# Attention in another order with the output projection and the layer norms between its halves, and feed-forward tiles at other addresses

## The chip, the cores and the metric

One core of one Trainium2 chip runs the whole program. TensorE (PE) multiplies, VectorE (DVE), ScalarE (ACT) and GpSimd (POOL) do the rest, SyncE (SP) issues the DMAs. A kernel's time is device microseconds of one execution; the profile comes from one execution with its own time. Operands of matmuls stand in SBUF, where each of 128 partitions has its own bytes; "an address" below is a byte offset in every partition. Results go to PSUM.

## The reference

One layer of a decoder trunk: 2048 tokens, width 1024. An input projection feeds four causal mixers of 256 columns each (RWKV-7, dilated attention, Mamba-2 SSD, HGRN2). Their joined output goes through an output projection and a layer norm, then through a feed-forward part of 4096 columns and a second layer norm:

```python
  proj = x @ W_in[l]
  y    = concat(rwkv7, dilated_attn, ssd, hgrn2) @ W_out[l]
  x    = LayerNorm(alpha * x + y)
  x    = LayerNorm(alpha * x + relu(x @ W_up)^2 @ W_down)
```

The attention has 4 heads of 64 and three branches, with window 128, 512 and 2048 and dilation 1, 4 and 16. Each branch takes every d-th token as a row of its own, cuts it into blocks of 128, and a block attends to itself and to the block before it, with a bias that falls linearly with distance. The branches are merged by their softmax sums:

```python
    s = einsum(qb, kb) * (Dh ** -0.5) + bias
    m = max(s); p = exp(s - m); l = sum(p)
    o = einsum(p, vb) / l
```

## The kernel before

**Arithmetic.** Every large product is taken in three: an operand is split into a high and a low part (tiles ending in `h` and `l`, from `split`, `split_to` or `tsplit`), and high x high, high x low and low x high are summed in PSUM. A matmul of this kind has 512 moving columns and takes its 128x128 stationary operand in a load of its own (PEld).

**Order.** The program is written in one order and a scheduler, when the program is built, sets from it the order of each engine's instructions; the chip then works each engine's list off in turn, waiting on semaphores. Tiles come from pools; a tile with `bufs=n` has n places and waits for the reader of the one n tiles back. Six PSUM banks (`bank` in the profile) are given out by name with `slot`, two more are the pool `pd` (tile `mm`).

**Stages.** First the input projection and the mixers RWKV, HGRN and SSD run, to about 1265 us; the change leaves them. Then:

- *Attention* (`attn_units`, `attn_unit`): 48 units, one for each branch, remainder and block of 128 queries. A unit has two halves (`par`, two heads each). A half multiplies queries and keys (4 heads' worth in two calls, `kT`, `qT`; 128 or 256 keys), adds the bias and takes the maximum on DVE (`aS`, `aml`), takes the exponential on ACT, transposes on PE, copies to `aPT` on ACT or DVE, multiplies with the values (`av`, called PV below) and copies to `ao`, which a DMA stores to `od`. The first 12 units use other PSUM banks (`"1"`) and stand in the program while the last mixer still runs.
- *First part of the output projection* (`out_part(t)`, 16 tiles of 128 tokens): loads three mixers' output `ym`, transposes it (6 transposes), splits it to `yh`, `yl`, multiplies with 6 of the 8 row tiles of the weights (36 matmuls), adds alpha times x in `zt`, and stores that to `zF`.
- *Closing part* (`out_final(t)`): loads the three branches (`mo`), merges them (`attn_merge`, on POOL and DVE with `me`, `md`, `mw`), transposes and splits to `yah`, `yal`, multiplies with the last two row tiles (12 matmuls), does the layer norm (`stat`, and on ACT a square that is only wanted for its sum, into `junk`), stores it to `x1`, transposes it (8 transposes) into `x1t` and stores that to `x1T`, from which the feed-forward part reads.
- *Feed-forward up* (`ffn_up(hf, ...)`, two halves of 1024 tokens): seven products in place of eight, after Strassen, for 16 steps `s`, with 84 matmuls each. `ffn_x(hf)` builds the seven sums of activations `X` once for each half of the tokens, from loads `xr`; `ffn_w(s)` builds the sums of weights (`wr`, `wh`, `wl`). The finished columns go to `HT`.
- *Feed-forward down* (`ffn_down`): 3072 matmuls and the second layer norm.

The body (lines 1403 to 1424 of the kernel before) puts these in the order: units 12 to 47; parts 0 to 7; then, for t from 0 to 7, final t and part 8 + t; then the feed-forward part, with finals 8 to 15 behind the steps 1 to 8 of its first half. The scheduler weaves part of this: in the trace, parts 0 to 7 stand among the halves, and so do some finals.

The tiles of the feed-forward part come from the pools `fx` (activations in the up stage, all operands in the down stage), `fr` (raw loads) and `fw` (weights in the up stage, from the other end of SBUF). In the built program the `fx` tiles start 160 bytes past a multiple of 2048, and the 512-byte slices of a weight tile that serve as stationary operands start 480 bytes past a multiple of 512.

## Time and profile before

| | |
|---|---|
| median of 3 runs | 3184.59 us (3163.18 to 3186.83) |
| profiled execution, own time | 3170.08 us |
| its span | 3168.3 us |
| mean granted TensorE clock | 0.938 |
| attention starts in earnest | 1268 us |
| first steady up matmuls | 1820 us |
| down stage | 2461.6 to 3158.4 us |

A row of the stretches below gives start and end, length, then for each engine its busy time with the number of its instructions, the granted clock of TensorE (1.00 is full speed), the share of time in which a DMA engine was busy, and GB/s. The busy time of PE counts overlapping matmuls once; the length of a single matmul in a row of the timeline is from its start to its last result, so the pace is read from the starts.

### The profile page before, as it was taken

The numbers are of one execution on the slowest core, as the hardware profiler recorded it, in microseconds if no ns is written. First come the engines' busy times: TensorE is split into PE (matmuls) and PEld (weight loads), VectorE is DVE, ScalarE is ACT, GpSimd is POOL, SyncE is SP. The second block draws the span as 40 slices with busy tenths as digits, with TensorE's granted clock in tenths as the row PEclk, the third lists the DMA queues.
The fourth block names the chain that finished last, engine by engine and source line by source line (L and its number), as shares of the span: only waits on it lengthen the run. The fifth ranks groups of instructions, "written<-read, shape, count | busy, mean of one in ns | idle before, by whom it ended". The sixth has DMA issues, their size and how long they took to land.

```text
span 3168.3 us, 44820 instructions
## 1 busy us (share of the span) xinstructions
PE 2988.8 (94%) x15908; PEld 2418.1 (76%) x15908; DVE 1803.9 (57%) x3577; ACT 1170.1 (37%) x2566; POOL 1063.2 (34%) x1115
## 2 busy tenths in 40 slices
PE   8899988989899998999998799998999999999998
PEld 6667777777677787777776588876888888888887
DVE  3457589687877855433354755565444333333348
ACT  3335334433443432433442454455445211111113
POOL 1333466365555645100123743344232111111111
PEclk9899898989999998798698899998999999999999
DMA  5343323432343344432256544433333622222213
GB/s 174 125 120 106 110 91 97 126 101 74 114 120 101 111 142 156 140 126 96 81 171 196 168 130 146 137 119 121 108 109 106 223 74 77 76 73 74 74 60 117
DMA packets 260145, 369.92 MB, mean 117 GB/s; under 512 B 27600, under 2 KB 145488, under 8 KB 259664
## 3 DMA queue, kind: packets, MB, share of 16 engines
q1 hardware_dynamic: 259920, 367.04, 36.8%
q8 instruction: 126, 2.06, 0.3%
q14 instruction: 99, 0.81, 0.1%
HBM read 256.12 MB, written 110.82 MB: 116 GB/s over the span
## 4 chain that ended last, share of the span: by engine, by line
PE 69%; DVE 14%; DMA 8%; issue 3%; POOL 3%; ACT 2%; SPq 1%; DVEq 0%; POOLq 0%; ACTq 0%
PE bank L112 52%; PE mm L112 15%; PE bank L157 2%; DMA xraw<-in_xT 2%; DVE hgQ L115 2%; DVE rzp L115 1%; DVE rZc L115 1%; DVE stg L128 1%; DVE wl L115 1%; DMA raw<-in_w_ch 1%; DVE xl L115 1%; DMA rLB<-lcd 1%; DMA od<-ao 1%; DMA hqP<-chF 1%; DVE hqP L115 1%
## 5 line engine op out<-in xcount | busy, mean ns | idle before, releaser
L112 PE MATMUL bank<-xl,xh 128*128 128x512 f32 x1024 | 398.3, 389 | 0.0
L112 PE MATMUL bank<-xh,xh 128*128 128x512 f32 x1024 | 398.3, 389 | 0.0
L112 PE MATMUL bank<-xh,xl 128*128 128x512 f32 x1024 | 398.0, 389 | 0.0
L112 PE MATMUL bank<-xh,wh 128*128 128x512 f32 x896 | 358.5, 403 | 12.7 <-ACT xh L135 7.6
L112 PE MATMUL bank<-xl,wh 128*128 128x512 f32 x896 | 359.8, 402 | 7.7 <-DVE xl L115 6.0
L112 PE MATMUL bank<-xh,wl 128*128 128x512 f32 x896 | 357.3, 399 | 0.0
L112 PE MATMUL mm<-xh,wh 128*128 128x512 f32 x672 | 284.0, 425 | 29.9 <-ACT xh L135 16.6
L112 PE MATMUL mm<-xl,wh 128*128 128x512 f32 x672 | 283.1, 421 | 6.3 <-POOL xl L115 3.8
L112 PE MATMUL mm<-xh,wl 128*128 128x512 f32 x672 | 279.7, 416 | 3.7 <-DVE wl L115 3.6
L112 PEld LDWEIGHTS bank<-xh,xl 128*128 128x128 f32 x1024 | 192.3, 188 | 39.9
L112 PEld LDWEIGHTS bank<-xl,xh 128*128 128x128 f32 x1024 | 192.3, 188 | 39.9
L112 PEld LDWEIGHTS bank<-xh,xh 128*128 128x128 f32 x1024 | 192.3, 188 | 39.8
L128 DVE SCALAR_TENSOR_TENSOR y<-y,bank 128x512 f32<-128x512 f32 x160 | 109.4, 686 | 196.1 <-PE bank L112 191.6
L112 PEld LDWEIGHTS bank<-xh,wh 128*128 128x128 f32 x896 | 170.3, 190 | 60.5 <-ACT xh L135 13.2
L112 PEld LDWEIGHTS bank<-xl,wh 128*128 128x128 f32 x896 | 170.6, 190 | 54.9 <-DVE xl L115 11.0
L135 ACT ACTIVATE wh<-raw 128x512 fp32r<-128x512 f32 (+1 forms) x220 | 136.9, 629 | 193.0 <-PE mm L112 85.6
L112 PEld LDWEIGHTS bank<-xh,wl 128*128 128x128 f32 x896 | 170.6, 190 | 40.2
L112 PEld LDWEIGHTS mm<-xh,wh 128*128 128x128 f32 x672 | 133.5, 199 | 69.3 <-ACT xh L135 21.6
L135 ACT ACTIVATE wh<-wr 128x512 fp32r<-128x512 f32 x160 | 100.7, 630 | 176.9 <-PE bank L112 163.0
L115 DVE TENSOR_TENSOR wl<-raw,wh 128x512 fp32r<-128x512 f32 (+1 forms) x146 | 116.7, 803 | 85.6 <-ACT wh L135 83.8
L112 PEld LDWEIGHTS mm<-xl,wh 128*128 128x128 f32 x672 | 134.1, 200 | 40.6 <-POOL xl L115 5.8
L112 PEld LDWEIGHTS mm<-xh,wl 128*128 128x128 f32 x672 | 134.1, 200 | 36.0 <-DVE wl L115 5.2
(403 smaller groups left out, 6552.4 us busy)
## 6 DMA issues: line engine op xcount, KB each, us to landing
raw<-in_w_ch SPq DMA_DIRECT2D x140, 256.0 KB, 3.0
wr<-in_w_up SPq DMA_DIRECT2D x128, 256.0 KB, 3.2
chF<-stg SPq DMA_DIRECT2D x68, 256.0 KB, 2.4
xraw<-in_xT SPq DMA_DIRECT2D x64, 256.0 KB, 3.7
HT<-u SPq DMA_DIRECT2D x64, 256.0 KB, 3.5
xr<-in_w_down SPq DMA_DIRECT2D x64, 256.0 KB, 2.9
xh<-HT SPq DMA_DIRECT2D x128, 128.0 KB, 2.5
xl<-HT SPq DMA_DIRECT2D x128, 128.0 KB, 2.6
```

The source lines that it names most:

```text
L112: self.nc.tensor.matmul(out, lhsT, rhs, start=start, stop=stop)
L115: (self.nc.gpsimd if eng == "g" else self.nc.vector).tensor_tensor(out, a, b, op=op)
L128: self.nc.vector.scalar_tensor_tensor(out, a, s, b, op0=op0, op1=op1, **kw)
L135: self.nc.scalar.activation(out, in_, AF.Copy)
L157: self.nc.tensor.transpose(out, in_, self.ident[:n, :n])
```

## The change

**Order of the units.** `attn_units` sorts them: the 16 units of dilation 16 first (each of one block; the first 12 units of all have `"1"`, as before), then dilation 1 and 4 by turns, by the stretch of 512 tokens in which they lie. So four tiles of 128 tokens have all three branches as soon as their stretch is through. The bias table `abias` gets two buffers, `aS` two in place of three.

**Weaving.** `attn_unit`, `out_mm`, `out_part` and `out_final` become generators: the first stops after each half, at its last PV matmul, a part stops 7 times, a final once. The new function `weave(units, fills)` walks through the halves and between them lets so many steps of the fills run that both end together; each step is tied behind the PV matmul of the half before (`issue_after`), so that the scheduler puts it no earlier. Four weaves: units 12 to 23 with parts 0 to 6; 24 to 31 with parts 7 to 10 and finals 0 to 3; 32 to 39 with parts 11 to 15 and finals 4 to 7; 40 to 47 with finals 8 to 11, with `ffn_x(0)` written ahead of these. Finals 12 to 15 stand behind steps 1 to 4 of the up stage.

**Small edits.** The square in `out_final` writes to `x1t` (one buffer) and no `junk`. `ffn_x` loads the first four operands ahead, reads some of them again in place of keeping them, and has 24 loads for the first half of the tokens and 20 for the second, where there were 16 for each. In the down stage 22 sums `y2` have places of their own, before 20.

**Addresses.** A tile `top` of 1888 bytes stands below `fr` and `fx`, one named `pad` of 2016 bytes beside `fw`, and `fr` stands ahead of `fx`. In the built program both kinds of operand then start at a multiple of 2048 (moving) and of 512 (stationary) in both feed-forward stages. All matmuls are the same in number and shape.

```diff
     def attn_units(self):
...
-                            st["bias"] = self.t(self.aw, "abias", [P, NH, 256], bufs=1)
+                            st["bias"] = self.t(self.aw, "abias", [P, NH, 256], bufs=2)
...
-                    out.append(go)
-        return out
+                    out.append(((n * d // 4, b, r, n) if d < 16 else (-1, b, r, n), go))
+        return [go for _, go in sorted(out, key=lambda x: x[0])]
...
-            S = self.t(aw, "aS", [P, 2, 256], bufs=3)
+            S = self.t(aw, "aS", [P, 2, 256], bufs=2)
...
-        nc.sync.dma_start(dst, o)
+            if par:
+                nc.sync.dma_start(dst, o)
+            yield pv.ins
+
+    def weave(self, units, fills):
+
+        n, done, pv = sum(c for _, c in fills), 0, None
+        steps = (x for f, _ in fills for x in f)
+        for i, last in enumerate(x for un in units for x in un()):
+            while done < n * (i + 1) // (2 * len(units)):
+                with self.tc.issue_after(pv or last):
+                    next(steps)
+                done += 1
+            pv = last
+        with self.tc.issue_after(pv):
+            for _ in steps:
+                pass
...
     def out_final(self, t, tag=None):
...
-        junk = self.t(op, "junk", [P, D], BF16)
-        self.lnorm(zt, stat, junk, self.ln1[:, 0, :], self.ln1[:, 1, :])
+        xt = self.t(op, "x1t", [P, KT, P], bufs=1)
+        self.lnorm(zt, stat, xt.rearrange("p k n -> p (k n)"), self.ln1[:, 0, :], self.ln1[:, 1, :])
...
     def ffn_open(self, es):
         tc = self.tc
+        top = es.enter_context(tc.tile_pool(name="top", bufs=1))
+        self.t(top, "top", [P, 472])
+        self.fr = es.enter_context(tc.tile_pool(name="fr", bufs=1, reuse_waits="tile"))
         self.fx = es.enter_context(tc.tile_pool(name="fx", bufs=1, reuse_waits="tile"))
-        self.fr = es.enter_context(tc.tile_pool(name="fr", bufs=1))
...
         for k in range(4):
...
+            put("B11", ld(k, 0, 0))
+        if hf == 0:
+            for k in range(4):
+                put("B21", ld(k, 1, 0))
+        for k in range(4):
+            b12, t1, b22 = ld(k, 0, 1), ld(k, 0, 0), ld(k, 1, 1)
+            self.sub("v", t1, b12, t1)
+            self.sub("g", b12, b22, b12)
             put("B22", b22)
...
-    for un in units[12:]:
-        un()
-    half = nt // 2
-    for t in range(half):
-        B.out_part(t)
-    for t in range(half):
-        B.out_final(t, "tp")
-        B.out_part(half + t)
+    part = lambda t: (B.out_part(t), 7)
+    final = lambda t: (B.out_final(t, "tp"), 1)
+    B.weave(units[12:24], [part(t) for t in range(7)])
+    B.weave(units[24:32], [f(i) for t in range(4) for f, i in ((part, 7 + t), (final, t))])
+    B.weave(units[32:40], [f(i) for t in range(4) for f, i in ((part, 11 + t), (final, 4 + t))] + [part(15)])
     eo.close()
+    B.ffn_open(ef)
+    X = B.ffn_x(0)
+    B.weave(units[40:], [final(8 + t) for t in range(4)])
     ea.close()
-    B.ffn_open(ef)
     with ExitStack() as e1:
-        B.fw = pool("fw", e1, side="right")
-        for hf in range(2):
-            B.ffn_up(hf, lambda s: B.out_final(half + s - 1) if hf == 0 and 0 < s <= half else None)
+        B.t(pool("pad", e1, side="right"), "pad", [P, 504])
+        B.fw = pool("fw", e1, side="right", reuse_waits="tile")
+        B.ffn_up(0, X, lambda s: run(B.out_final(11 + s)) if 0 < s < 5 else None)
+        B.ffn_up(1, B.ffn_x(1), lambda s: None)
     B.ffn_down()
```

**On PE, among the halves.** The rows are PE's instructions in their order: line, operation, output and inputs, shape. `kT,qT` are scores, `ident,aS` the transposes of a half, `av,aPT` its PV, `ident,ym` and `wh,yh` those of a part, `ident,z` of a final. Before, behind the last matmul of part 7:

```order
L112 MATMUL bank_62<-av_12948,aPT_12978 128x64 x2
L157 MATMUL bank_65<-ident,aS_13033 128x128 x4
L112 MATMUL bank_62<-av_12984,aPT_13000 128x64 x4
L157 MATMUL bank_66<-ident,aS_13053 128x128 x4
L112 MATMUL bank_62<-av_12984,aPT_13020 128x64 x4
L112 MATMUL bank_63<-kT_12027,qT_12025 128x128
L112 MATMUL bank_63<-kT_12028,qT_12026 128x128
L112 MATMUL bank_62<-av_13028,aPT_13044 128x64 x4
```

Only halves follow there. In the change, in the third weave:

```order
L112 MATMUL bank_62<-av_14886,aPT_14902 128x64 x4
L157 MATMUL bank_65<-ident,aS_15036 128x128
L157 MATMUL mm_14637<-ident,ym_14631 128x128 x4
L157 MATMUL mm_14644<-ident,ym_14631 128x128 x2
L157 MATMUL bank_65<-ident,aS_15036 128x128
L157 MATMUL bank_66<-ident,aS_15083 128x128 x4
L112 MATMUL bank_62<-av_14886,aPT_14936 128x64 x4
L112 MATMUL bank_63<-kT_12027,qT_12025 128x256
L112 MATMUL bank_63<-kT_12028,qT_12026 128x256
L112 MATMUL bank_62<-av_15031,aPT_15047 128x64 x4
L157 MATMUL bank_61<-ident,z_2508_14593 128x128 x4
L112 MATMUL mm_14674<-wh_12537,yh_14635 128x512
```

Between two halves there now stand the six transposes of a part, those of a final's result, or a few of its matmuls.

**On PE, at the start of the feed-forward part.** The products of the up stage read `xh`, `xl`. Before, from the end of a final's matmuls (`yah`):

```order
L112 MATMUL mm_16275<-wh_12627,yah_16257 128x512
L112 MATMUL mm_16275<-wl_12628,yah_16257 128x512
L112 MATMUL mm_16275<-wh_12627,yal_16258 128x512
L112 MATMUL bank_61<-xh_15766,wh_15936 128x512
L112 MATMUL bank_61<-xl_15767,wh_15936 128x512
L112 MATMUL bank_61<-xh_15766,wl_15937 128x512
L157 MATMUL mm_16292<-ident,z_2845_16264 128x128 x4
L157 MATMUL mm_16298<-ident,z_2845_16264 128x128 x4
```

In the change:

```order
L112 MATMUL mm_15874<-wh_12627,yal_15858 128x512
L112 MATMUL bank_62<-av_16106,aPT_16142 128x64 x4
L157 MATMUL bank_61<-ident,z_2776_15863 128x128 x8
L157 MATMUL bank_61<-ident,ya_15989 128x128 x2
L112 MATMUL bank_62<-xh_15464,wh_16248 128x512
L112 MATMUL bank_62<-xl_15465,wh_16248 128x512
L112 MATMUL bank_63<-xh_15429,wh_16252 128x512
L112 MATMUL bank_63<-xl_15430,wh_16252 128x512
L112 MATMUL bank_62<-xh_15464,wl_16249 128x512
L112 MATMUL bank_64<-xh_15468,wh_16256 128x512
```

The last halves stand now just ahead of the first products, which go to several banks in turn.

**On SP, the loads for the first operands.** `xr` are the loads of X, `wr` weights, `x` with a number a store of a final's result, `mo` the branches that a final merges. Before:

```order
L1116 DMA zt_15405<-in_x 128x1024
L1168 DMA xr_15764<-x1T_12520 128x512
L1111 DMA ym_15522<-ymix_0_90 128x256
L1111 DMA ym_15522<-ymix_1_91 128x256
L1111 DMA ym_15522<-ymix_2_92 128x256
L507 DMA od_12045<-ao_14108 128x264
L1193 DMA wr_15928<-in_w_up 128x512
L1134 DMA x_4_12492<-z_2624_15213 128x1024
```

In the change:

```order
L440 DMA mo_2829_16151<-od_12045 128x264
L440 DMA mo_2831_16155<-od_12047 128x264
L1192 DMA xr_15421<-x1T_12520 128x512
L1192 DMA xr_15427<-x1T_12520 128x512
L1192 DMA xr_15433<-x1T_12520 128x512
L474 DMA av_16062<-vF 128x2x256
L1192 DMA xr_15439<-x1T_12520 128x512
L509 DMA od_12046<-ao_15903 128x264
L1192 DMA xr_15445<-x1T_12520 128x512
L1192 DMA xr_15451<-x1T_12521 128x512
```

The loads of X stand among the attention's own loads and stores (`av`, `od`) and come ahead of the weights.

65 lines of the change are left out of this document (30 added, 35 removed).

## The prediction

> **What bounds the kernel now.** I read the page first, then the chain of waits in order of time, then the busy time by stretches, and last the same stretches for single tiles. From the page, the span, the busy times, the granted clock in 40 slices of 79 us, and the shares of the chain that ended last:
>
> ```profile
> span 3168.3 us, 44820 instructions
> PE 2988.8 (94%) x15908; PEld 2418.1 (76%) x15908; DVE 1803.9 (57%) x3577; ACT 1170.1 (37%) x2566; POOL 1063.2 (34%) x1115
> PEclk9899898989999998798698899998999999999999
> PE 69%; DVE 14%; DMA 8%; issue 3%; POOL 3%; ACT 2%; SPq 1%; DVEq 0%; POOLq 0%; ACTq 0%
> ```
>
> PE is busy 94% of the span and carries 69% of the chain. The clock has its low slices (7, 8, 6, 8) at the 18th to 22nd slice, which is 1340 to 1740 us, the attention. The change leaves the mixers before that as they are, so I look from 1268 us on. The chain there (start, length, what):
>
> ```profile
> 1752.86 6.23 DMA x1T<-x1t
> 1759.10 2.73 DMA xr<-x1T
> ...
> 1820.49 76.06 PE bank L112 x326
> ...
> 2164.66 990.83 PE bank L112 x4323
> ```
>
> A store of x1T and a load back from it stand on the chain just before the feed-forward part runs; from 1820 us on it is PE alone, with breaks. The busy time by stretches (start and end, length, PE, PEld, DVE, ACT, POOL with counts, granted clock, DMA share, GB/s):
>
> ```profile
> 1268.00:1340.00 72.00, 65.77 (x309) 54.56 (x309) 36.48 (x147) 35.31 (x128) 14.12 (x14) 0.69 0.39 126
> 1340.00:1461.00 121.00, 120.62 (x579) 92.85 (x578) 39.87 (x171) 40.43 (x161) 0.00 (x0) 0.96 0.40 130
> 1461.00:1565.00 104.00, 101.74 (x427) 81.11 (x425) 34.23 (x166) 42.12 (x158) 6.91 (x24) 0.59 0.24 74
> 1565.00:1651.00 86.00, 84.76 (x483) 67.70 (x481) 47.05 (x159) 38.11 (x124) 20.33 (x52) 0.98 0.52 162
> 1676.00:1755.00 79.00, 63.77 (x275) 48.60 (x274) 40.44 (x82) 19.88 (x42) 34.41 (x59) 0.89 0.58 185
> 1755.00:1820.00 65.00, 48.17 (x161) 31.48 (x160) 54.14 (x76) 28.89 (x55) 52.12 (x59) 0.84 0.58 184
> 2109.00:2166.00 57.00, 46.49 (x168) 33.50 (x167) 46.29 (x48) 30.39 (x54) 37.18 (x25) 0.88 0.43 134
> 2170.00:2400.00 230.00, 230.00 (x987) 185.32 (x986) 111.59 (x163) 113.14 (x191) 68.40 (x50) 1.00 0.33 109
> 2461.60:3158.40 696.80, 696.59 (x3074) 576.63 (x3072) 301.59 (x514) 140.60 (x249) 87.99 (x76) 1.00 0.29 93
> ```
>
> To know what runs in each, the same stretches for the tiles `aml` (one DVE operation for each attention half), `yh` (24 matmuls for each first part of the output projection, "part" below) and `yah` (8 for each closing part, "final"):
>
> ```profile
> 1268.00:1340.00 72.00, 3.15 (x19) 16.45 (x76) 0.69 0.39 126
> 1340.00:1461.00 121.00, 4.13 (x27) 24.99 (x108) 0.96 0.40 130
> 1461.00:1565.00 104.00, 4.25 (x28) 28.39 (x112) 0.59 0.24 74
> 1565.00:1651.00 86.00, 3.12 (x18) 18.68 (x72) 0.98 0.52 162
> ```
>
> ```profile
> 1268.00:1340.00 72.00, 8.19 (x24) 4.43 (x24) 1.01 (x2) 1.29 (x3) 0.69 0.39 126
> 1340.00:1461.00 121.00, 57.34 (x167) 32.17 (x167) 7.47 (x14) 6.39 (x14) 0.96 0.40 130
> 1565.00:1651.00 86.00, 24.91 (x72) 12.86 (x72) 3.29 (x6) 2.89 (x6) 0.98 0.52 162
> 1676.00:1755.00 79.00, 31.79 (x96) 18.28 (x96) 4.34 (x8) 3.75 (x8) 0.89 0.58 185
> ```
>
> ```profile
> 1565.00:1651.00 86.00, 8.58 (x25) 5.19 (x25) 1.27 (x3) 1.10 (x3) 0.98 0.52 162
> 1676.00:1755.00 79.00, 13.28 (x34) 7.49 (x32) 1.68 (x4) 1.54 (x4) 0.89 0.58 185
> 1755.00:1820.00 65.00, 8.98 (x25) 5.23 (x24) 1.23 (x3) 1.10 (x3) 0.84 0.58 184
> ```
>
> So 19 halves and a part; then 27 halves and 7 parts at a clock of 0.96; then 28 halves alone at 0.59; then 18 halves, 3 parts and 3 finals at 0.98; then 4 parts and 4 finals alone; then 3 finals and the start of the feed-forward part, which DVE (54 of 65 us) and POOL (52) hold back. The slow places are the 104 us of bare attention and the 144 us from 1676 to 1820, where PE has gaps of 32 us.
>
> **The change part by part.** Prices first. At full clock one 512-column matmul in the down stage takes 696.8/3072 = 226.8 ns, in the up stage 230/987 = 233.0 ns. At half clock four of them that follow one another start within 1.28 us, 0.427 apart, and four transposes take 0.53 us (start, length; the next start ends it):
>
> ```profile
> 1421.77 0.63 PE L112 MATMUL mm<-wh,yl 128*128 128x512 f32 x1
> ...
> 1423.05 0.63 PE L112 MATMUL mm<-wh,yl 128*128 128x512 f32 x1
> ...
> 1462.15 0.61 PE L157 MATMUL bank<-ident,aS 128*128 128x128 f32 x4
> 1462.68 0.55 PE L112 MATMUL bank<-av,aPT 128*128 128x64 f32 x3
> ```
>
> A part has 36 matmuls and 6 transposes: 36 x 0.227 + 6 x 0.13 = 9.0 us. A final has 12 and 10: 12 x 0.227 + 1.3 = 4.0 us. A woven half is what is left of a stretch: (86 - 3 x 9.0 - 3 x 4.0)/18 = 2.6 us from 1565; (121 - 7 x 9.0)/27 = 2.15 us from 1340, where about half of them have one key block and not two. Alone a half takes 104/28 = 3.7 us, beside the last mixer (72 - 9)/19 = 3.3 us.
>
> *The order.* The first 24 halves now run without parts: 24 x 3.3 = 79 us, to 1347. First weave, 24 halves of one- and two-block units with 7 parts: 24 x 2.15 + 63 = 115, to 1462. Second, 16 halves with 4 parts and 4 finals: 16 x 2.6 + 4 x 13.0 = 94, to 1556. Third, the same and a part: 103, to 1659. Fourth, 16 halves with 4 finals and the first operands X of the feed-forward part: PE needs 16 x 2.6 + 16 = 58, but DVE needs 16 x 34.23/28 = 19.6 for the halves, and 54.1 for X and finals (the stretch from 1755 has both, with 3 finals for 4): I take 75, to 1734. A short stall at the first product, 6 us: 1740. Before, PE ran steadily from 1820; of the up matmuls some 95 were then done, since 63 read `xh`, as two of three do:
>
> ```profile
> 1755.00:1820.00 65.00, 26.08 (x63) 13.41 (x63) 17.59 (x18) 15.89 (x27) 13.82 (x9) 0.84 0.58 184
> ```
>
> With finals 0 to 10 and most of 11 done as well, the equal point is 1820 - 95 x 0.233 = 1798. The weave gains 58 us. Its ends: if the 32 halves of the second and third weave cost the 3.7 of bare ones, 35 less, and if X comes behind the halves and not beside them, 20 less still: 3. If woven halves all cost 2.15 (32 x 0.45 = 14) and X hides wholly (75 to 58), 31 more, and the stall's 6 go away: 95. I take 58, since both prices are from rows with the same mixture.
>
> What moves with the parts and finals counts too: their loads and stores on SP's queue, and the merges on POOL. The stretch from 1565 has both beside halves, with DMA at 0.52 and POOL at 20 of 86 us, so two of the weaves cost no more than it; in the fourth, X brings POOL to the 52 us of the stretch from 1755, less than the 75 for DVE, and its loads stand in SP's queue between the halves' own.
>
> *Operand addresses.* Before, both operands of the down stage start 160 bytes past a multiple of 512 (the moving one of 2048); of the up stage the moving one does and the stationary one lies 480 past. Afterwards all are at 0. No trace shows that. The nearest row is the down stage, where both have the same remainder: I take the up stage (2 x 16 x 84 = 2688 matmuls) from 233.0 to the 226.8 of that, 2688 x 6.2 ns = 17 us, and nothing for the down stage. The ends are a loss of 3072 x 6.2 = 19 us, if 0 is the worse remainder and the down stage goes to 233.0, and a gain of 2688 x 19.5 + 3072 x 13.3 = 93 us, if all come at half of the 0.427 of the half clock, 213.5 ns. By the Trainium skill, "TensorE: Matmul & The Clock Gate", section "Back-to-back issue gap", a lone 512-column matmul has a gap of 518 cycles, 215.7 ns; by that figure this term would be 80 us for both stages, and no row here is that short.
>
> *The middle of the up stage.* X for the second half of the tokens is built from 20 loads and not 16, with its first four operands ahead. The stretch from 2109 holds 168 matmuls, 39.1 us at 0.233, in 57: 17.9 us of stall. The first operands come sooner and DVE does the same work; I take 5 of it, ends 0 and 17.9.
>
> *At nothing.* The new loads (12 of 256 KB, 2.7 us each by the chain) go to a DMA that is 0.58 busy at most; the PE stream covers them, and if not each costs its 2.7. The square of a final now writes `x1t`, of which there is one buffer, so it waits for the store before it (6.2 us); behind it on ACT stand the exponentials and copies of later halves, but finals come some 23 us apart. With the cover gone that is 6 us for each of 16. `abias` with two buffers, `aS` with two for three, `y2` in two more fixed tiles: no wait of their size in the list of the bare stretch, where DVE waits for `aS` because of the store of `ao` instead (us in total, times, longest):
>
> ```profile
> DVE aS L486 <- DMA od<-ao: 27.3, 11, 3.3
> ACT aS L131 <- DVE aml L490: 18.1, 10, 4.3
> ```
>
> That store comes now once for each unit behind its second half; it waits as before.
>
> Sum: 58 + 17 + 5 = 80. The profiled execution took 3170.1 us, 1.8 more than its span, so 3090. The median of the three runs, 3184.6, lies 14.5 above it; from there it would be 3105. About 1%, 32 us, is what a measurement of this kernel tells from no change.
>
> **The rivals.** *Addresses do nothing* (3107). The projections at the start, whose operands lie at other remainders again, come at 232 ns (eleven in a row, the first and the last shown: 10 gaps in 2.32 us), so that 233 may be the common pace:
>
> ```profile
> 59.81 0.39 PE L112 MATMUL mm<-xh,wh 128*128 128x512 f32 x1
> ...
> 62.13 0.39 PE L112 MATMUL mm<-xl,wh 128*128 128x512 f32 x1
> ```
>
> Against it: the same instruction at the same clock takes 226.8 in one stage and 233.0 in the other, steadily. By the Trainium skill, "SBUF — State Buffer", section "Who interferes with whom", PE reads its two operands through independent ports and waits for nobody, so that no address would matter; the two stage rows don't agree with that simply.
>
> *Both stages stream with nothing between* (3013). If the remainder costs every matmul here, not only those with unlike ones, the down stage gains too: 3090 - 5760 x 13.3 ns = 3013. For it: at half clock 0.427 is 512 columns and no more. Against: no row at full clock shows it.
>
> *The softmax sets the pace* (3145). DVE, ACT and the stores pass each half on; if 3.7 us is their latency and not the clock's, the weave fills gaps but not the chain: 3090 + 35 + 20. For it: the waits of `aS`, 45 us in the 104. Against: 2.6 us in the stretch with everything.
>
> *Slower: the clock stays at half in the woven stretch* (3306). The bare attention ran so though PE was busy throughout:
>
> ```profile
> 1520.00:1540.00 20.00, 20.00 (x81) 16.02 (x82) 5.56 (x28) 6.72 (x27) 0.00 (x0) 0.50 0.23 68
> ```
>
> The fills are now cut into pieces of 6 or so matmuls between small attention ones. If that counts as attention does, 16 x 36 + 12 x 12 = 720 matmuls cost 0.2 us more, 144, and the 56 halves of the first three weaves 3.7 each, 24 x 1.55 + 32 x 1.1 = 72: 216 in all. It decides the sign once 80/216 = 37% of the stretch is at half clock. Against: 0.96 and 0.98 where parts were woven in before.
>
> **How the numbers follow.** Forecast 0.40, addresses nothing 0.22, both stages short 0.17, softmax 0.12, half clock 0.06, other 0.03. The likeliest gives 3090. The range 3005 to 3150 takes in the first four cases, with the stall's and the stage's ends and the 15 us between median and profiled run, and leaves out the last two and the tails, some 0.15. Faster by over 1% are the first three, 0.79, and a little of the fourth: 0.81; within 1% the rest of it and mixtures, 0.11; slower 0.08.
>
> **What would show it.** A clock of 0.9 or more from 1350 to 1740 and no stretch of halves alone; the first steady up matmul near 1740 and DVE nearly full in the 70 us ahead of it; 230 us of up matmuls holding some 1014 and not 987; 697 us for the down stage (656 if the second rival holds); a stall of 13 at the change of halves. I am wrong if the woven stretch shows gaps on PE as large as before, or if the up stage keeps its 233.

## The result, and the profile after

The changed kernel takes 3150.0 us, the median of 8 executions (3133.6 to 3159.9); the kernel before, timed in the same rounds, 3176.8 (3155.7 to 3193.4). The ratio is 0.991, 95% interval 0.988 to 0.994: some 27 us less, where 80 were forecast. A gain of 0.9% lies just under the 1% that the prediction named as the bound of what can be told from no change, but the interval leaves no change out. The profiled execution took 3152.4 us.

From the page of the changed kernel, the span, the busy times, the granted clock in slices of 79 us, and the chain's shares:

```profile
span 3150.6 us, 44927 instructions
PE 2974.9 (94%) x15908; PEld 2419.7 (77%) x15908; DVE 1806.8 (57%) x3577; ACT 1174.8 (37%) x2566; POOL 1060.4 (34%) x1115
PEclk9899798987999999679999799998999999999999
PE 71%; DVE 13%; DMA 7%; issue 3%; POOL 3%; ACT 2%; SPq 1%; DVEq 0%; POOLq 0%; ACTq 0%
```

The stretches from the first half of the attention on, cut at what happens in this trace (start and end, length, PE, PEld, DVE, ACT, POOL with counts, granted clock, DMA share, GB/s):

```profile
1285.70:1354.80 69.10, 65.94 (x273) 53.39 (x272) 30.07 (x137) 32.40 (x124) 8.05 (x8) 0.53 0.25 83
1354.80:1464.00 109.20, 107.80 (x537) 87.41 (x536) 37.66 (x167) 39.87 (x154) 0.00 (x0) 0.89 0.38 125
1464.00:1585.00 121.00, 121.00 (x624) 94.40 (x622) 59.06 (x202) 47.94 (x157) 24.12 (x71) 0.96 0.46 150
1585.00:1667.00 82.00, 81.76 (x399) 64.59 (x398) 36.47 (x117) 29.73 (x90) 14.09 (x32) 0.92 0.53 165
1667.00:1724.00 57.00, 56.00 (x312) 45.30 (x313) 33.62 (x116) 28.27 (x84) 18.71 (x44) 1.00 0.53 165
1724.00:1754.00 30.00, 17.25 (x104) 13.03 (x101) 19.31 (x40) 15.46 (x42) 17.42 (x18) 0.83 0.78 239
1754.00:1807.40 53.40, 40.56 (x140) 29.31 (x140) 40.30 (x70) 20.99 (x42) 46.60 (x66) 0.77 0.58 178
...
2105.90:2158.50 52.60, 34.61 (x85) 20.11 (x84) 24.77 (x32) 19.74 (x35) 22.91 (x17) 0.68 0.36 105
2158.00:2400.00 242.00, 242.00 (x1069) 200.36 (x1069) 124.38 (x183) 124.55 (x211) 78.76 (x57) 1.00 0.35 117
2444.00:3140.20 696.20, 696.20 (x3073) 576.47 (x3072) 305.92 (x513) 141.72 (x249) 87.74 (x75) 1.00 0.28 93
```

The weave does what it says: the 104 us of bare attention are gone, PE has next to no gap from 1355 to 1724 and the clock is 0.89 to 1.00 there. Then come 83 us, to 1807, in which PE has gaps of 25 us and a clock of 0.83 and 0.77 (before, from 1676 to 1820, gaps of 32 us and 0.89 and 0.84); and a hole at the change of token halves, 85 matmuls in 52.6 us. The up stage goes at 242/1069 = 226.4 ns, the down stage as it did.

**The ledger of the two profiled executions** (starts of PE's instructions). The difference of the spans is 17.7 us:

| from, to | before | changed | gain |
|---|---|---|---|
| start to the first half's scores | 1269.9 | 1285.7 | -15.8 |
| first half's scores to the 169th up matmul | 567.7 | 541.5 | +26.2 |
| from there to the first down matmul | 624.1 | 616.9 | +7.2 |
| of it: the first 84 up matmuls of the second token half | 37.7 | 52.7 | -15.0 |
| the rest | 706.6 | 706.5 | +0.1 |

The first line is not the change's. Up to about 1150 us the two kernels have the same instructions in the same order on PE, DVE, ACT and POOL; some 15 us of the difference are there by then, and they come in a few places where one execution was granted less clock. The same 103 matmuls, before and then changed, with PE busy throughout both times:

```profile
732.20:747.20 15.00, 15.00 (x103) 10.75 (x102) 9.40 (x25) 5.64 (x17) 6.07 (x8) 0.97 0.40 81
```

```profile
737.40:760.90 23.50, 23.50 (x103) 17.11 (x104) 9.06 (x24) 5.66 (x17) 6.03 (x8) 0.57 0.37 64
```

That is half of the 15.8 us. Executions of one kernel lie 25 to 40 us apart, and the long ones were granted less clock: of the changed kernel, 3133.6 us at a mean of 0.943 and 3159.9 us at 0.931. Without that line the traces differ by 33 us; the medians by 27. So there are three things to explain: 26 us from the weave for 58, 15 us lost at the change of halves for 5 gained, and whether the addresses did their part.

### The profile page after: what moved, and what is told of

The parts are those of the page before. It is cut to its first block, busy times and chain, and to the rows that moved or that the text cites. A ratio compares the mean times of both kernels' runs of the same rounds, so it can differ in the third digit from the quotient of the medians.

```text
span 3150.6 us, 44927 instructions
## 1 busy us (share of the span) xinstructions
PE 2974.9 (94%) x15908; PEld 2419.7 (77%) x15908; DVE 1806.8 (57%) x3577; ACT 1174.8 (37%) x2566; POOL 1060.4 (34%) x1115
## 3 DMA queue, kind: packets, MB, share of 16 engines
q1 hardware_dynamic: 261648, 370.19, 37.3%
## 4 chain that ended last, share of the span: by engine, by line
PE 71%; DVE 13%; DMA 7%; issue 3%; POOL 3%; ACT 2%; SPq 1%; DVEq 0%; POOLq 0%; ACTq 0%
PE bank L112 53%; PE mm L112 16%; PE bank L157 2%; DMA xraw<-in_xT 2%; DVE hgQ L115 2%; DVE stg L128 1%; DVE rzp L115 1%; DVE wl L115 1%; DVE rZc L115 1%; DMA raw<-in_w_ch 1%; DVE xl L115 1%; DMA chF<-stg 1%; DMA xr<-x1T 1%; DMA hqP<-chF 1%; ACT xh L135 1%
## 5 line engine op out<-in xcount | busy, mean ns | idle before, releaser
L112 PE MATMUL bank<-xh,wh 128*128 128x512 f32 x896 | 354.3, 398 | 18.7 <-ACT xh L135 17.1
L112 PE MATMUL mm<-xh,wh 128*128 128x512 f32 x672 | 284.2, 425 | 33.2 <-ACT xh L135 18.5
L128 DVE SCALAR_TENSOR_TENSOR y<-y,bank 128x512 f32<-128x512 f32 x176 | 120.5, 686 | 224.6 <-PE bank L112 221.0
L135 ACT ACTIVATE xh<-xr 128x512 fp32r<-128x512 f32 x120 | 72.6, 626 | 272.3 <-PE bank L112 194.4
L115 DVE TENSOR_TENSOR wl<-raw,wh 128x512 fp32r<-128x512 f32 (+1 forms) x146 | 124.9, 859 | 71.5 <-ACT wh L135 65.3
L112 PE MATMUL mm<-wh,xh 128*128 128x256 f32 (+1 forms) x512 | 156.2, 308 | 5.0 <-ACT stg L131 3.6
```

What stands on the lines that cost most here:

```text
L112: return self.nc.tensor.matmul(out, lhsT, rhs, start=start, stop=stop)
L115: (self.nc.gpsimd if eng == "g" else self.nc.vector).tensor_tensor(out, a, b, op=op)
L128: self.nc.vector.scalar_tensor_tensor(out, a, s, b, op0=op0, op1=op1, **kw)
L135: self.nc.scalar.activation(out, in_, AF.Copy)
```

## The experiments

Five readings of each trace are compared. **A** is the time from the first half's scores to the 169th up matmul (11 to 13 of the finals lie in it, 13 in the change, 12 before, 11 in late_four_mixed; each is some 4 us of PE). **P** is the start of the last matmul of part 15. **X** is the first and last of the 28 splits of the first X on ACT. **B** is the time from the last half's scores to the 85th up matmul. **C** is the time of the first 84 up matmuls of the second token half, and its stall over 84 times the pace. All in us; "ratio" to the kernel before, with 95% interval, where it was timed in rounds. One kernel was profiled twice (`mixed_x`, `mixed_timed`): B differs by 0.0, C by 0.4, A by 8, again by clock.

| run | ratio | A | P | X | B | C, stall |
|---|---|---|---|---|---|---|
| before | 1 | 567.7 | 1750.9 | 1752.5 to 1814.4 | | 37.7, 18.1 |
| the change | 0.991 (0.988 to 0.994) | 541.5 | 1713.2 | 1715.6 to 1808.3 | 83.3 | 52.7, 33.6 |
| four_bufs | 0.993 (0.991 to 0.996) | 554.8 | 1710.0 | 1715.4 to 1789.2 | 98.4 | 42.7, 23.7 |
| old_x | 0.995 (0.992 to 0.998) | 567.1 | 1705.2 | 1710.6 to 1783.7 | 106.8 | 36.9, 17.9 |
| x_from_input | | 551.5 | 1711.1 | 1713.5 to 1813.1 | 94.2 | 52.7, 33.6 |
| pool_light | | 550.6 | 1712.0 | 1714.4 to 1804.3 | 91.1 | 53.0, 34.0 |
| late_finals | 0.995 (0.992 to 0.997) | 545.9 | 1695.6 | 1699.3 to 1801.3 | 84.5 | 52.2, 33.2 |
| early_parts | 1.008 (1.006 to 1.011) | 597.5 | 1662.0 | 1665.3 to 1831.9 | 123.9 | 52.0, 33.0 |
| mixed_x | | 540.0 | 1700.9 | 1703.4 to 1796.1 | 83.4 | 35.8, 16.7 |
| mixed_timed | 0.986 (0.983 to 0.989) | 548.4 | 1713.1 | 1715.5 to 1808.5 | 83.4 | 36.2, 17.1 |
| late_four_mixed | 0.984 (0.981 to 0.988) | 529.9 | 1694.0 | 1699.6 to 1772.6 | 75.4 | 34.2, 15.2 |
| dense_third | 0.985 (0.982 to 0.987) | 537.5 | 1697.8 | 1700.2 to 1794.8 | 84.4 | 37.3, 18.2 |
| dense_both | 1.007 (1.004 to 1.010) | 602.4 | 1678.8 | 1682.2 to 1864.1 | 130.8 | 36.0, 17.0 |
| junk_back | 0.989 (0.984 to 0.994) | 557.5 | 1698.4 | 1703.8 to 1802.4 | 95.0 | 37.9, 18.9 |
| align | 1.007 (1.004 to 1.010) | 593.5 | 1782.4 | 1786.4 to 1849.1 | | 38.1, 19.0 |
| x1t_only | | 595.7 | 1781.0 | 1782.7 to 1847.0 | | 35.6, 16.0 |
| ya_only | | 565.0 | 1755.2 | 1762.7 to 1819.0 | | 37.2, 17.6 |

### What holds up X: first round

After the result I had three theories of the 83 us. *Buffers*: X has three raw buffers `xr` where it had four (three and `xt`), so that its loads wait. *POOL*: from 1754 POOL is busy 46.6 of 53.4 us. *The stores*: X waits for the eighth final's `x1T`, which lands about 1715.

**four_bufs.** A fourth buffer at the same tile addresses; the merge is done in place to make room.

```diff
-        ya = self.t(op, "ya", [P, 256], bufs=1)
-        self.attn_merge(t, op, ya)
+        ya = self.attn_merge(t, op, None)
...
-        self.t(top, "top", [P, 472])
+        self.t(top, "top", [P, 216])
...
-            raw = self.t(self.fr, "xr", [P, 512], bufs=3)
+            raw = self.t(self.fr, "xr", [P, 512], bufs=4)
```

> Four raw buffers for the loads xr in place of three, at the same tile addresses (the space comes from merging the attention in place). Two stretches are read: from the scores of the last attention half to the 85th up matmul (1724.1 to 1807.4 in the changed kernel, 83 us), and the first 84 up matmuls of the second token half (52.6 us, of which 33.6 are stall). If the three buffers hold up both builds of X, the first falls to about 65 us and the stall to about 18, and the time by some 30 us. If POOL's work sets the first and the buffers only the second, the first stays above 78, the stall falls to about 18, and the time by 15. If neither, both stay within 3 us.

**old_x.** The first and second X as they were built before.

> The changed kernel with X built as before: 16 loads and not 24 or 20, one buffer for the difference beside three for the loads, tile addresses as in the change. If the new order of X's loads costs the 33.6 us of stall at the change of halves, it falls back to about 18 us (17.9 before), the time by some 15 us or more. If instead the stall is larger only because the products before it now run faster, it stays above 28. At the start, a theory of POOL's work expects little change (both orders have 8 subtractions on POOL): 78 to 88 us from the last scores to the 85th up matmul; one of the loads expects under 70.

**x_from_input.** No load of the first X waits for a store.

```diff
-            self.nc.sync.dma_start(raw, self.xT[2 * hf + l][4 * i + k])
+            self.nc.sync.dma_start(raw, self.xT[2 * hf + l][4 * i + k] if hf else self.ap["xT"][(4 * i + k) * P : (4 * i + k + 1) * P, 512 * l : 512 * l + 512])
```

> The changed kernel, but X of the first token half is loaded from the layer's input and not from the first layer norm's result, so that the up stage works on other numbers; the same loads, none of which waits for the stores of x1T. If the wait for the eighth final's store (x1T landed about 1715 us) is what puts X behind the halves, X is built beside them and the 85th up matmul comes some 40 us earlier, the 83 us fall to 50 or less. If POOL or the buffers set its pace once it starts, it comes earlier by less than 15 us.

**pool_light.**

```diff
-            self.sub("g", b12, b22, b12)
+            self.sub("g" if hf else "v", b12, b22, b12)
...
-            self.sub("g", b21, b21, b22)
+            self.sub("g" if hf else "v", b21, b21, b22)
```

> The eight subtractions of the first X that POOL does (1.54 us each, 12.3 us) are given to DVE (0.69 each). From 1754 to 1807 us POOL is busy 46 of 53 us in the changed kernel. If POOL sets the pace there, the 83 us fall by 8 to 12; if the three buffers or the loads do, by less than 4; the change of halves, where nothing is moved, keeps its stall of 33.6.

*What came.* At the change of halves the theory of buffers and loads holds: the stall of 33.6 us falls to 23.7 with a fourth buffer and to 17.9 with the old order, and does not move in the other two. What ACT waited for loads of X at the change of halves (us in total, times, longest), before (2086 to 2166 us) and in the change (2086 to 2158):

```profile
ACT xh L135 <- DMA xr<-x1T: 6.4, 2, 3.3
```

```profile
ACT xh L135 <- DMA xr<-x1T: 24.8, 9, 3.6
```

At the start none of the three holds as put. POOL with 12 us less work made B longer by 8, not shorter. X from the input began no sooner, at 1713.5 us, though its first three loads were issued 420 us ahead. On SP in x_from_input and in the change:

```profile
1293.62 1.28 SPq L1192 DMA_DIRECT2D xr<-in_xT  x3
```

```profile
1612.35 1.27 SPq L1192 DMA_DIRECT2D xr<-x1T  x3
```

In both, three raw buffers were full and the splits waited for something else. Four buffers did shorten X, from 93 to 74 us, and so did the old order (73), but B grew from 83 to 98 and 107: PE now waited longer for a layer norm's result, whose transposes stand in its list ahead of the up matmuls. The waits of PE's loads for it (us in total, times, longest) in the change and in four_bufs:

```profile
PEld bank L157 <- DVE z L128: 7.9, 2, 6.4
```

```profile
PEld bank L157 <- DVE z L128: 25.7, 3, 13.0
```

Four_bufs and old_x also merge the attention in place, which was run alone only in the order of before; whether that makes the finals later here is not shown. And x_from_input and pool_light have 94 and 91 for 83 with no buffer more, so a difference of 10 us in B carries little.

And in all four, X's first split on ACT came 2 to 6 us behind the last matmul of part 15 (columns X and P). That gave the next theory: the pool `fx` is opened when the pools of the parts are closed, and its tiles lie on the memory of the projection's weights and the parts' tiles. So `xh` and `xl` can't be written before part 15 is through with that memory. The raw buffers lie elsewhere: in the built program of the change they stand where the weights were loaded, while the first three `xh` stand on a weight (`wh_12537`), a `yh` and a `ym` of the parts.

### Part 15, the finals' chain, and X's own length

**late_finals.** Is it the finals 8 to 12, one behind the other, that fill the 83 us?

```diff
-    B.weave(units[40:], [final(8 + t) for t in range(4)])
+    B.weave(units[40:], [])
...
-        B.ffn_up(0, X, lambda s: run(B.out_final(11 + s)) if 0 < s < 5 else None)
+        B.ffn_up(0, X, lambda s: run(B.out_final(7 + s)) if 0 < s < 9 else None)
```

> The changed kernel with finals 8 to 11 taken out of the fourth weave: finals 8 to 15 stand behind steps 1 to 8 of the up stage, as in the kernel before. Theory of the finals' chain (their layer norms follow one another some 20 us apart, and PE's list has their transposes ahead of the up matmuls): the 83 us from the last scores to the 85th up matmul fall to about 45, and the time by some 25 us once the four finals are paid behind the steps at 4 us each. Theory that X itself (28 splits, 16 subtractions, three raw buffers) takes its 93 us however little stands beside it: the stretch stays above 70 and the time as it is or worse.

B is 84.5, but the run does not do what the edit says. The scheduler put finals 9, 10 and 11 into the stretch all the same, though they stand behind the steps in the program; only final 12 left it. The matmuls that read `yah` (8 for each final) from the last half's scores to the 85th up matmul, in the change and in late_finals:

```profile
1724.10:1807.40 83.30, 12.87 (x32) 7.97 (x32) 1.65 (x4) 1.49 (x4) 0.80 0.65 200
```

```profile
1713.80:1798.30 84.50, 7.69 (x24) 4.36 (x24) 1.26 (x3) 1.52 (x4) 0.74 0.58 180
```

What did go is PE's wait for a layer norm's result: 1.3 us in all for 7.9, while that for `xh` rose from 5.6 to 16.4. So PE no longer waits for a final but for X, and the stretch is as long as before. What the finals' work on DVE and POOL costs X is not shown. X's splits take 102 us here, and their groups show how. For each of four `k`, the first split (of `B22`), three together (`T2`, `T1`, `T3`) and one (`T4`); starts on ACT in late_finals:

```profile
1722.46 0.63 ACT L135 ACTIVATE xh<-xr 128x512 fp32r<-128x512 f32 x1 [0.39 <-DMA xr<-x1T]
1725.85 1.67 ACT L135 ACTIVATE xh<-xr 128x512 fp32r<-128x512 f32 x3
1732.64 0.63 ACT L135 ACTIVATE xh<-xr 128x512 fp32r<-128x512 f32 x1 [0.74 <-POOL xr L115]
1740.01 0.63 ACT L135 ACTIVATE xh<-xr 128x512 fp32r<-128x512 f32 x1 [0.45 <-DMA xr<-x1T]
1745.70 1.67 ACT L135 ACTIVATE xh<-xr 128x512 fp32r<-128x512 f32 x3 [1.97 <-DVE xr L115]
...
1767.27 1.67 ACT L135 ACTIVATE xh<-xr 128x512 fp32r<-128x512 f32 x3 [2.71 <-DVE xr L115]
...
1789.78 1.67 ACT L135 ACTIVATE xh<-xr 128x512 fp32r<-128x512 f32 x3 [1.14 <-DVE xr L115]
```

The groups of three stand 20 to 23 us apart, and what ends each wait is a load or a subtraction. With three buffers `b12`, `t1` and `b22` fill the ring; `b21` can be loaded only when `T3` has been split off `b12`, and the next three only behind that. A group is one chain of loads, subtractions and splits with nothing ahead of it.

**early_parts.** All parts in the first two weaves, so that part 15 ends early, and X's place in the program as it was.

```diff
-    B.weave(units[12:24], [part(t) for t in range(7)])
-    B.weave(units[24:32], [f(i) for t in range(4) for f, i in ((part, 7 + t), (final, t))])
-    B.weave(units[32:40], [f(i) for t in range(4) for f, i in ((part, 11 + t), (final, 4 + t))] + [part(15)])
+    B.weave(units[12:24], [part(t) for t in range(10)])
+    B.weave(units[24:32], [f(i) for t in range(4) for f, i in ((part, 10 + t), (final, t))] + [part(14), part(15)])
+    B.weave(units[32:40], [final(4 + t) for t in range(4)])
```

> The changed kernel with all parts in the first two weaves (10 and 6), so that the third has finals 4 to 7 alone. X's tiles lie in the memory of the output projection's weights and of the parts' tiles, and in all four runs so far the first of X on ACT came 2 to 6 us behind the last matmul of part 15. If that memory is what puts X behind the halves, X starts here as soon as its loads allow, with most of the 16 halves of the fourth weave still to come, and the stretch from the last scores to the 85th up matmul falls from 83 to 50 or less; the time falls by 10 to 30 us. If X's place is set by the order of the program or by the stores of x1T, the stretch stays above 75.

Part 15 ended at 1662, and X began at 1665, with 20 halves still to come. But only its first eight splits could run, which come from tokens of finals 0 to 3; the ninth waited for final 7, whose matmuls end at 1753 here. On ACT in early_parts:

```profile
1681.55 0.63 ACT L135 ACTIVATE xh<-xr 128x512 fp32r<-128x512 f32 x1 [1.84 <-DMA xr<-x1T]
1772.88 0.63 ACT L135 ACTIVATE xh<-xr 128x512 fp32r<-128x512 f32 x1 [0.41 <-DMA xr<-x1T]
```

So X waits for two things, the memory of the parts and the stores of final 7, and whichever comes last decides. In the change they come together, part 15 at 1713 and final 7's last transposes at 1709. The time rose by 0.8%: the third weave, with only four finals among 16 halves, ended late (the last half's scores come 453 us behind the first's, 438 in the change), and final 7 with it.

**dense_third and dense_both** (on the kernel of mixed_x, below) end the parts sooner in another way: the fills of the third weave, or of the second and third, between half as many halves.

```diff
-    B.weave(units[32:40], [f(i) for t in range(4) for f, i in ((part, 11 + t), (final, 4 + t))] + [part(15)])
+    B.weave(units[32:36], [f(i) for t in range(4) for f, i in ((part, 11 + t), (final, 4 + t))] + [part(15)])
...
+    B.weave(units[36:40], [])
     B.weave(units[40:], [final(8 + t) for t in range(4)])
```

> The second X as before (as in the run that took 3128 us), and the fills of the third weave put between 8 halves and not 16, so that part 15 ends sooner and 24 halves stand behind X in the program and not 16. If X waits for the memory of the parts' tiles, X's first split follows part 15 by 2 to 6 us again, comes 15 to 25 us before 1713, and more halves lie beside X: the time from the first half to the 169th up matmul (541.5 us in the change) falls by 10 to 25. If X's place follows from the program's order or PE has to carry the halves anyway, it falls by less than 5.

> The same for the second weave too: its fills between 8 halves, then parts 11 to 15 between 8, finals 4 to 7 between 8, and X. By the theory of the memory part 15 ends some 50 us sooner and X starts its first 8 splits then, but the rest waits for the stores of final 7; the time from the first half to the 169th up matmul falls by 10 to 40. If the dense fills make DVE or the finals' chain late, it rises instead, as it did by 56 us when all parts stood in the first two weaves.

dense_third was a weak test. Counted from the first half's scores, part 15 ended at 422 us where it was 427 in the change, and X with it; A is 537.5, within what clock alone does. The same 90 halves still stood ahead of part 15: the fills were let go sooner, but PE did the waiting halves in between all the same. dense_both ended part 15 at 387, X began 3.4 us behind it, and its ninth split waited for final 7 as in early_parts; A rose to 602.

### The change of halves

**mixed_x and mixed_timed.** The second X as before, with `xt` in 2 KB that are free there; the first X, and everything ahead, as in the change.

```diff
+        if hf:
+            for k in range(4):
...
+                t = self.t(self.fr2, "xt", [P, 512], bufs=1)
+                self.sub("v", t, b12, b11)
+                put("T1", t)
...
+        B.fr2 = pool("fr2", e1, side="right")
         B.ffn_up(0, X, lambda s: run(B.out_final(11 + s)) if 0 < s < 5 else None)
```

> The changed kernel with X of the second token half built as before (16 loads, one more buffer for the difference, in 2 KB that are free there); the first X as in the change. If buffers and loads make the 33.6 us of stall at the change of halves, it falls to 18, by 15, and the rest of the trace is as in the change: 83 us, give or take 10, from the last scores to the 85th up matmul.

> The second X built as before, the rest as in the change, timed in rounds: one look gave 3125 us and a stall of 16.7 in place of 33.6. If that is all, the ratio to the kernel before is 0.991 less 17/3170, about 0.986.

Both came as expected: C goes back to 36 us, and the ratio is 0.986, though its interval (0.983 to 0.989) just overlaps that of the change (0.988 to 0.994). In mixed_x the row that answers to the 52.6 us of the change is

```profile
2093.70:2129.50 35.80, 25.20 (x85) 15.94 (x85) 29.09 (x31) 18.53 (x33) 25.16 (x16) 0.94 0.38 125
```

**late_four_mixed.** Finals 8 to 11 behind the steps, as in late_finals, and four raw buffers, and the second X as in mixed_x (with `xt`). It merges in place too.

> Both things that stand at the start of the feed-forward part taken away at once: finals 8 to 11 behind the up steps, and four raw buffers for X; X of the second half as before, with one buffer more. With three buffers X's 28 splits took 86 to 102 us from first to last, in groups of 22 us, with four 74; with four buffers alone PE waited 26 us in place of 8 for the layer norms' results, and with the finals alone moved X's 102 us were still there. If two chains of much the same length run side by side, the stretch from the last scores to the 85th up matmul falls here from 84 to 55 to 65, and the time to about 3100. If a third thing (PE's half clock, weights, DVE) sets it, it stays above 75 and the time near that of the second X alone, 3125.

B is 75.4, not 55 to 65, so the forecast of two chains missed its size. X takes 73 us, from 1699.6 to 1772.6, and the 85th up matmul starts 8 us behind its last split. As in late_finals the finals did not all go: of 9 to 12, 9 and 10 run in the stretch. PE waits 1.9 us for a layer norm's result there, 7.2 for `xh` and 7.9 for a weight, `wh`. From the last scores to there, DVE is busy 58 of 75 us and POOL 59:

```profile
1705.60:1781.00 75.40, 53.33 (x186) 38.77 (x185) 58.05 (x90) 33.71 (x74) 59.20 (x63) 0.73 0.53 172
```

What of the 73 us is still buffers, and what the two engines' work or the two finals', no run tells. Over mixed_timed the ratio is better by 0.0014 (0.9844 for 0.9858), which is less than either interval: most of what late_four_mixed has over the change is the second X.

### The addresses

**align.** The kernel before, its order and loops, with tiles at the change's addresses.

```diff
+        self.t(es.enter_context(tc.tile_pool(name="top", bufs=1)), "top", [P, 216])
         self.fx = es.enter_context(tc.tile_pool(name="fx", bufs=1, reuse_waits="tile"))
...
+        B.t(pool("pad", e1, side="right"), "pad", [P, 504])
         B.fw = pool("fw", e1, side="right")
```

> The kernel before with the tile addresses of the change alone (both operands of both stages at a multiple of 2048 or 512; the space for it from the square in x1t and the merge in place). The trace of the change gives 226.7 ns for the up stage where it was 233.3, and 226.7 for the down stage as before. Addresses as the cause: 226.7 here too, and 15 to 20 us less than before. Order as the cause (fewer of other engines' accesses beside the matmuls): 233 and no gain.

**mv0_st480 and mv160_st0** leave out `pad`, or take another `top`, so that only one operand moves.

> The kernel before with the moving operands of the up stage at a multiple of 2048, the stationary ones still 480 past a multiple of 512 (the down stage has both at 0). If the stationary operand's remainder costs the 6.6 ns, the up stage keeps 233.3 ns; if the moving one's, it has 226.7; if each has a share, something between. Only the paces are read, not the time.

> The other way round: the stationary operands of the up stage at a multiple of 512, the moving ones still 160 past a multiple of 2048 (the down stage as before, both at 160). If the stationary operand's remainder costs it, 226.7 ns in the up stage; if the moving one's, 233.3.

200 us of the up stage in align, mv0_st480 and mv160_st0:

```profile
2200.00:2400.00 200.00, 200.00 (x884) 165.59 (x883) 98.79 (x145) 100.54 (x169) 61.70 (x45) 1.00 0.34 113
```

```profile
2200.00:2400.00 200.00, 200.00 (x859) 160.67 (x858) 97.15 (x142) 98.38 (x166) 60.36 (x44) 1.00 0.34 112
```

```profile
2200.00:2400.00 200.00, 200.00 (x855) 160.77 (x854) 97.22 (x140) 99.33 (x169) 62.02 (x46) 1.00 0.34 112
```

Read from the starts over eight steps, a matmul takes:

| moving past 2048, stationary past 512 | us stage | ns |
|---|---|---|
| 160, 480 (before) | up | 233.3 |
| 0, 480 | up | 233.3 |
| 160, 0 | up | 234.3 |
| 0, 0 (align, the change) | up | 226.7 |
| 160, 160 (before, mv160_st0) | down | 226.7 |
| 0, 0 (align, mv0_st480, the change) | down | 226.7 |

It is neither operand alone. Both at the same remainder give 226.7 ns, at 0 or at 160; unlike ones 233.3 or 234.3. That the addresses and not the order did it, align shows. By the Trainium skill, "SBUF — State Buffer", section "Who interferes with whom", PE reads its two operands through independent ports and waits for nobody: what is measured here is a cost of 3% that goes with how the two lie to each other, and the measurement decides. By the Trainium skill, "TensorE: Matmul & The Clock Gate", section "Back-to-back issue gap", a lone matmul of 512 columns has a gap of 518 cycles, measured there as 215.7 ns; none of the rows here is that short.

**What made align slower.** Its up stage is faster, and the kernel 0.7% slower: A is 593.5 us where the kernel before has 567.7. Two small edits had made room for the pads, the square into `x1t` and the merge in place.

```diff
-        junk = self.t(op, "junk", [P, D], BF16)
-        self.lnorm(zt, stat, junk, self.ln1[:, 0, :], self.ln1[:, 1, :])
+        xt = self.t(op, "x1t", [P, KT, P], bufs=1)
+        self.lnorm(zt, stat, xt.rearrange("p k n -> p (k n)"), self.ln1[:, 0, :], self.ln1[:, 1, :])
```

> The kernel before with the square of the layer norm written to x1t (one buffer) and not to a tile of its own. Priced at nothing in the prediction, since finals come some 23 us apart. If it costs nothing, the time from the first half to the 169th up matmul stays at 568 us, give or take 8; if it is what made three runs with the order of before slower, it is 585 or more, and the change carries that cost too.

> The kernel before with the merged attention written in place of the first branch and not to a tile of its own (used in some runs to make room; not in the change). If this made the three runs slower, the time from the first half to the 169th up matmul is 585 us or more and that of the square in x1t is 568; otherwise it is 568, give or take 8.

It is the square: 595.7 alone, against 565.0 for the merge (one execution each; A is 591.8 and 591.9 in mv0_st480 and mv160_st0, which have both edits). The prediction had it at nothing, and the change has it too, so the separate tile was put back into the changed order:

> The change with the second X as before (timed: 3128 us), and in it the square of the layer norm in a tile of its own again; the space comes from merging in place, which alone left the kernel before as it was (565 us for 568 from the first half to the 169th up matmul). If the square in x1t costs the change what it costs the kernel before, that stretch, 540 to 548 us there, falls by 20 or more and the time to about 3105. If it only shifted the scheduler's order in the kernel before, where parts have no fixed place, the stretch stays within 8 us and the time at 3128.

There it brings nothing: A is 557.5 and B 95.0, no better than 540 to 548 and 83.4, and the ratio 0.989 (0.984 to 0.994) for 0.986. (The merge in place stands in this run too, and was not run alone in the changed order; a gain by the tile and a loss by the merge would look the same.) In the kernel before, the edit cost its 28 us by way of the order: from the first half to the first final's matmuls there are 324.1 us in x1t_only and 295.0 before, with parts 0 to 7 and 76 and 74 halves in them, and that lies ahead of the first square. With other tiles the scheduler wove the parts in other places, and the changed kernel, whose parts are tied to halves, has less freedom there. How it came to that order was not followed up.

## Why the prediction was right or wrong

**Prices of parts, finals and halves: right.** By the sum 96 halves, 16 parts and 8 finals are through 433 us after the first half (391 to the end of the third weave and 16 halves at 2.6); in the trace the last half's scores come after 438. The clock in the woven stretch is 0.89 to 1.00, where 0.9 or more was forecast.

**The fourth weave: the step that failed.** The prediction put X beside 16 halves and took 75 us for the two, from 391 us after the first half on, with DVE as the bound. In the trace 90 of the 96 halves lie ahead of the end of part 15, and six beside X (the tile `aml`, one DVE operation for a half):

```profile
1285.70:1713.50 427.80, 14.84 (x90) 88.14 (x360) 0.87 0.42 136
1713.50:1754.00 40.50, 1.52 (x6) 6.43 (x24) 0.88 0.75 233
```

Two things were overlooked. The weave holds the fills back and not the halves, so that ten halves of the fourth weave ran in among the parts of the third and part 15 ended after 427 us. And X's tiles lie on the parts' memory, so that X could not run ahead with the halves and began 2 us behind part 15, 39 us later than the sum had it; `ffn_open` stands in the diff right behind `eo.close()`, which gives that memory back, and the prediction took addresses only for the operands' remainders. The sum expected the 85th up matmul 466 + 6 + 19 = 491 us after the first half, the trace has it after 521.7: 30 us of the 58. The end that I had given, "X comes behind the halves and not beside them, 20 less", was nearly that case and too small: X with its three buffers took 93 us, with some five finals and six halves beside it, where X before took 62. A second tie that the prediction did not see, X's ninth split behind final 7, cost little here because final 7 and part 15 ended together. The two ties are shown by early_parts, dense_both and x_from_input. That the halves ran ahead is read from the trace alone: no run held them back until X could start, so what the weave would have gained then is not shown.

**The middle of the up stage: the wrong sign.** "I take 5 of it, ends 0 and 17.9." The stall grew from 18.1 to 33.6 us. The prediction counted 20 loads for 16 and did not count that the tile `xt` was gone, which leaves three raw buffers for a step that holds three at once. No reason excluded a loss, and yet the lower end stood at 0. With a fourth buffer alone the stall was 23.7, with the old build in mixed_x and mixed_timed 16.7 and 17.1: some 10 us are the buffer's, the other 6 or 7 the order and number of the loads.

**The addresses: right**, 2688 x 6.6 ns = 17.7 us by the pace, for 17, and for the reason of the row it was taken from (the stage with like remainders). The down stage stays, as taken. So the rival that addresses do nothing and the one that both stages stream without overhead are both out.

**At nothing.** `abias` and `y2` show no wait that grew. Before it writes `aS`, DVE waited 29 us in all of the attention for transposes (20 before), and 5 for the store of `ao`, said to stay (78 before): less together, with one buffer fewer. The loads of X were not covered: over both builds ACT, DVE and POOL waited 59 us for them, 43 of it at the change of halves; before it was 22 and 14. The square in `x1t` costs the changed kernel nothing that junk_back could show. (The page's clock digits 7, 8, 6 and 8 stand at the 17th, 19th, 20th and 22nd slice, from 1267 us on, and not at the 18th to 22nd; no sum hangs on it.)

**The rivals.** The half clock in the woven stretch did not come. "The softmax sets the pace" had the nearest time, 3145, and half of a mechanism: X behind the halves was its second term, but halves in the weave are not slow. The sum with the terms as measured is 28 (weave) + 17.7 - 15.5 = 30, against 33 by the two traces and 27 by the medians.

## What to carry to other kernels

Before pricing work "beside" other work, look at what its tiles lie on: a tile that takes the place of another waits for that one's last reader, wherever the program writes it, and a load into a free place does not help it. Count the buffers of a chain of loads against how many it holds at once; one buffer fewer and four loads more cost 15.5 us here, nearly the whole address gain. When a run is to take work out of a stretch, look in its trace whether the work went. And a weave that ties only the fills lets the work it weaves them into run ahead, so that the cover is used up before the work that needed it can start.

## What was not expected of the hardware

A 512-column matmul costs 226.7 ns where both operands lie at the same remainder of 512 bytes, and 233.3 to 234.3 where they don't, whichever of the two is off; five pairs of remainders were seen.

The granted clock differs between executions over the same instructions with PE always busy, as in the rows of the mixers above (103 matmuls in 15.0 and 23.5 us). It does so in the woven attention too. The same 400 or so matmuls of mixed_x and then of mixed_timed, which are one kernel:

```profile
1511.50:1589.90 78.40, 78.26 (x402) 60.38 (x402) 40.04 (x136) 32.69 (x104) 15.26 (x39) 0.96 0.54 174
```

```profile
1515.30:1602.90 87.60, 87.60 (x403) 68.24 (x402) 40.50 (x136) 32.97 (x105) 15.31 (x39) 0.82 0.49 155
```

That is 9 us, more than some of the edits tried here, and nothing of it is in the program.

A DVE subtraction of two operands in SBUF takes 0.66 us at the least and was stretched up to 1.8 us where POOL worked beside it: 16 of the first X took 1.27 us on average in four_bufs, with POOL busy 71 of 98 us. The splits `xl` on DVE in the change (minimum, median and longest, in ns) and in four_bufs (number, busy us, mean ns):

```profile
L115 DVE TENSOR_TENSOR xl<-xr,xh x18: 661/682/1661, 1718.9 to 1802.1; 128x512 fp32r<-128x512 f32 x18
```

```profile
L115 DVE TENSOR_TENSOR xl<-xr,xh 128x512 fp32r<-128x512 f32 x16 | 20.0, 1269 | 1.3 <-ACT xh L135 1.3
```

By the Trainium skill, "SBUF — State Buffer", section "Who interferes with whom", such an instruction contends with one of GpSimd that reads SBUF. The traces agree in that only splits with POOL beside them were stretched, but not all of those were: in the change the four with no POOL instruction beside them took 0.68 to 0.69 us, and of the nine with POOL busy throughout one took 1.66 and the others 0.66 to 0.69. Whether it is also why work moved from POOL to DVE bought nothing in pool_light was not shown.
